# Spreading rows of 1/rms and norm weights over the partitions: two products of 512 columns with split diagonals instead of four float32 products of 128

## The chip, the cores and the metric

The kernel runs on one core of a Trainium2 chip. The metric is the device time of one execution in microseconds, the median of several runs. The engines are called TensorE (PE in the rows; PEld is its weight load), VectorE (DVE), ScalarE (ACT), GpSimd (POOL) and SyncE (SP, which here only issues transfers). L308 is line 308 of the kernel before.

## What is computed

The reference is a trunk of two layers over two groups of tokens, `x_sample` (512 tokens) and `x_prompt` (1024 tokens), 1024 features wide, all in float32:

```python
def rms_norm(x, g):
    xf = x.astype(jnp.float32)
    y = xf * lax.rsqrt(jnp.mean(xf * xf, axis=-1, keepdims=True) + EPS)
    return (y * g.astype(jnp.float32)).astype(x.dtype)

def run_trunk(x):
    cos, sin = axial_rope_tables(x.shape[1])
    for i in range(DEPTH):  # 2
        j = i // 2
        if i % 2 == 0:
            x = x + fourier_mixer(x, norm_mix[i], fourier_w[j])
        else:
            x = x + attention_mixer(x, norm_mix[i], attn_w_qkv[j], attn_q_norm[j],
                                    attn_k_norm[j], attn_w_o[j], cos, sin)
        x = x + swiglu_ffn(x, norm_ffn[i], ffn_w_gate[i], ffn_w_up[i], ffn_w_down[i])
    return x
```

Each mixer and each feed-forward block begins with `rms_norm`; the attention also normalises every head of Q and K.

## The kernel before

The tokens stand in three blocks of 512: block 0 is the sample, 1 and 2 are the prompt. Inside the trunk a block is held with its features on the 128 partitions (8 chunks `dc` of 128) and its 512 tokens along the free axis. The feed-forward inner width is 2816, 22 chunks of 128.

Products of float32 matrices are made from two float32r parts each. `split` (lines 235 to 244) writes a high part with ScalarE, rounded to float32r, and a low part, source minus high part, with VectorE or GpSimd; with a gain, ScalarE multiplies by it and the low part is one `scalar_tensor_tensor`. `mm3` (lines 246 to 249) then runs three matmuls, high by high, high by low, low by high, into the same bank; these are the rows of L247, L248 and L249. Weights are loaded by SyncE, their high part is made by ScalarE (L278) and their low part by GpSimd (L279).

The norm is spread over partitions as follows. A sum of squares of the 512 tokens becomes a column: `rstd_cols` gives a tile `y` of 128 x 4, token by token on the partitions, by way of twelve small VectorE instructions (`rsqrt`, lines 281 to 293). What multiplies the block is a row, 512 tokens along the free axis, the same on all partitions. `in_rows` (line 302) makes that row: for each of the four columns of `y`, ScalarE scales the identity by it (a diagonal matrix, L307), and TensorE multiplies the diagonal by a matrix of ones (L308), in float32, 128 columns at a time, into one PSUM bank `r`. The diagonals are tiles of the rotating tag `t`, of which the main chain has 3 buffers (`tF`), the side chain 4 (`tX`) and `moving` 6 (`tT`); the same tags hold loaded chunks of the residual, squares, rotated heads and results on their way to memory.

`in_rows` is called: twice at the start for the gains of the Fourier mixer, and twice more for the prompt's; once at the end of the sample's mixer (`follow`, the row is copied to `first["r"]` and multiplies the gate and up products of the first feed-forward block); at the head of `normed` (line 339), which makes the split operand `h` of the next block, six times; in `qkv` for each of two K heads of three blocks (line 1030); and in `moving` (line 796), which makes the operands of the last stage, for two blocks.

The work runs as a main chain and a side chain. The main chain is the feed-forward loop of one block (`ffn`), the side chain prepares the next block: the prompt's mixer, Q, K and V, attention, output projection, norms. `weave` advances the two by turns by costs in microseconds that are written at the `yield`s, and a scheduler then lays out each engine's queue from what is ready, with the program's order as priority. `pinned` keeps an instruction in program order. The last stage (`ffn_pair`) runs the second layer's feed-forward for blocks 1 and 2 alone and calls `in_rows` nowhere. At the start `busy(36)` runs 36 products of ones by ones to warm TensorE.

Of the kernel before, what the change touches and what calls it, by code (L numbers as in the profile page):

```python
# [10 lines left out]
F32 = mybir.dt.float32  # L11
F32R = mybir.dt.float32r
I32 = mybir.dt.int32
AF = mybir.ActivationFunctionType
# [3 lines left out]
P = 128  # L18
D = 1024
NC = D // P  # L20
TB = 512
# [103 lines left out]
def trunk_kernel(ctx: ExitStack, tc: tile.TileContext, t: dict):  # L125
    nc = tc.nc
    act, dve, pool, pe, sp = nc.scalar, nc.vector, nc.gpsimd, nc.tensor, nc.sync

    cp = ctx.enter_context(tc.tile_pool(name="cp", bufs=1))
# [4 lines left out]
    def open_pool(name, **kw):  # L134
        opened[name] = tc.tile_pool(name=name, bufs=1, **kw)
        pools[name] = opened[name].__enter__()
        return pools[name]

    def close_pool(name):
        opened.pop(name).__exit__(None, None, None)  # L140
# [17 lines left out]
    def nm(s):  # L158
        uid[0] += 1
        return f"{s}_{uid[0]}"  # L160

    def tl(name, shape, dt, tag, pool_=None):
        pool_ = pool_ or pools["sbX" if tag[-1] in "XB" else "sbF"]
        return pool_.tile([P, *shape], dt, tag=tag, name=nm(name), bufs=BUFS[tag])
# [23 lines left out]
    def bank():  # L188
        return tl("c", [TB], F32, "c" + cur[0], pools["ps" + cur[0]])

    def bank2():
        return tl("a", [2, TB], F32, "gX", pools["psX"])
# [20 lines left out]

    ident = cp.tile([P, P], F32, name="ident")
    make_identity(nc, ident)
    ones = cp.tile([P, P], F32, name="ones")
    dve.memset(ones, 1.0)
    act.activation(col(1), ones[:, 0:1], AF.Square)
    gains = cp.tile([P, 34], F32, name="gains")
# [16 lines left out]
    def split(hi, lo, src, gain=None, eng=None):  # L236

        eng = eng or dve
        if gain is None:
            act.copy(hi, src)  # L240
            eng.tensor_tensor(lo, src, hi.bitcast(F32), op=ALU.subtract)  # L241
        else:
            act.activation(hi, src, AF.Copy, scale=gain)
            eng.scalar_tensor_tensor(lo, src, gain, hi.bitcast(F32), op0=ALU.mult, op1=ALU.subtract)
# [57 lines left out]
    def in_rows(y, temp=None, ps=None):  # L302

        r = bank() if ps is None else ps
        for j in range(4):
            dg = (temp or tmp)(P)
            act.activation(dg, ident, AF.Copy, scale=y[:, j : j + 1])  # L307
            pe.matmul(r[:, j * P : (j + 1) * P], ones, dg, start=True, stop=True)  # L308
        return r

    ss, rstd, resident = {}, {}, {}
# [23 lines left out]
    def normed(b, gain, got, ab, held=None):  # L335

        yield 2.0
        r = in_rows(rstd[b])
        h = h_tile(ab)
        yield 1.0  # L340
        for dp in range(NC // 2):
            for dc, ps in zip((2 * dp, 2 * dp + 1), sides()):
                if held is None:
                    x = tmp()
                    sp.dma_start(x, xres[b][:, dc, :])
                else:
                    x = held[dc]
                dve.tensor_tensor(ps, r, x, op=ALU.mult)
                split(h[:, 0, dc], h[:, 1, dc], ps, gain=gain[:, dc : dc + 1])
            yield 1.5  # L350
        got["h"] = h
# [66 lines left out]
    def mixer(seq, done, u, xrs, zz):  # L418
# [4 lines left out]
        if two:  # L423
            g2 = bank2()
            ga, gb = in_rows(gx[:, 0:4], ps=g2[:, 0]), in_rows(gx[:, 4:8], ps=g2[:, 1])
            sums = [x.rearrange("p (k n) -> p k n", k=2) for x in whole[seq]]
        else:
            ga, gb = done["gain"]
            sums = [h[:, i] for h in (tl("x", [2, 2, TB], F32, "wX") for _ in range(2)) for i in range(2)]
# [362 lines left out]
    def moving(blocks, gain, ops):  # L792

        tp = open_pool("tT")
        yield 2.0
        r = [in_rows(rstd[b], lambda n: tl("t", [n], F32, "tT", tp)) for b in blocks]
        yield 1.0
        for j in range(4):
            v = {}
            for k in range(2):  # L800
                for d in range(2):
                    c = 4 * d + j
                    x = tl("x", [TB], F32, "tT", tp)
                    sp.dma_start(x, xres[blocks[k]][:, c, :])
                    v[d, k] = x
            a2 = bank2()
            a, b = a2[:, 0], a2[:, 1]
            for (d, k), x in v.items():
                dve.scalar_tensor_tensor(
                    a if (d, k) == (0, 1) else x, x, gain[:, 4 * d + j : 4 * d + j + 1], r[k], op0=ALU.mult, op1=ALU.mult  # L810
                )

            def put(name, src, eng=None):
                split(ops[name][:, 0, j], ops[name][:, 1, j], src, eng=eng)

            def put_late(k, src):
                x = tl("l", [2, TB], F32R, "lT", tp)
                split(x[:, 0], x[:, 1], src, eng=pool)
                sp.dma_start(late[:, k, :, j, :], x.bitcast(F32))

            put("B11", v[0, 0], pool)
            put("B21", v[1, 0], pool)
            yield 6.0
            dve.tensor_tensor(b, a, v[0, 0], op=ALU.subtract)
            put("T1", b)
            dve.tensor_tensor(v[0, 1], v[1, 1], a, op=ALU.subtract)
            put_late(0, v[0, 1])
            put("B22", v[1, 1], pool)
            yield 6.0
            dve.tensor_tensor(b, v[1, 1], b, op=ALU.subtract)  # L830
            put("T2", b)
            dve.tensor_tensor(v[0, 0], v[1, 0], b, op=ALU.subtract)
            put_late(1, v[0, 0])
            yield 6.0
        close_pool("tT")
# [408 lines left out]
    def aux_3():  # L1244
        yield from paced(qkv(2, kept[2]), 0.4)
        yield from paced(attend((1, 2)), 0.65)
        for b in (1, 2):
            yield from paced(out_projection(b), 0.5)
        close_pool("ap")
        close_pool("sbX")  # L1250
        tp = open_pool("mT")
        for name in ("B11", "B21", "T2", "T1", "B22"):
            ops[name] = tl(name, [2, 4, TB], F32R, "mT", tp)
        yield from moving((1, 2), g_ffn[1], ops)
        close_pool("psX")
        last["pair"] = ffn_pair(1, (1, 2), ops, t["y"])
        cur[0] = "F"
        v = next(last["pair"])
        cur[0] = "X"
        yield v  # L1260
# [102 lines left out]
```

## Time and profile before

| | us |
|---|---|
| median of 3 runs | 3044.05 (3040.32 to 3046.63) |
| the profiled execution | 3041.73 |
| its span, first to last instruction | 3040.0 |
| TensorE with a matmul in flight | 2967.5 (98%) |
| VectorE busy | 1667.8 (55%) |
| GpSimd busy | 1282.6 (42%) |
| ScalarE busy | 1231.3 (41%) |

A share of busy time is a mean over stages. Matmuls overlap, so the pace of TensorE is read from the distance of starts and not from durations. A row of the timeline gives start, duration, engine, line, operation, what it writes and reads, the shape, the count of instructions merged in it, and in brackets the idle time of the engine before it and what ended that. An instruction that waits for a semaphore at the head of its queue holds all that is queued behind it on that engine.

### The profile page before, as it was taken

How to read it: one execution, taken by the hardware profiler on the slowest of the kernel's cores; microseconds unless marked ns; L12 is line 12 of the kernel's file. 1: busy time of each engine (PE TensorE's matmuls, PEld its weight loads, DVE VectorE, ACT ScalarE, POOL GpSimd, SP SyncE). 2: the span in 40 equal slices, each digit the busy share in tenths (PEclk: the TensorE clock that was granted, in tenths of full speed). 3: DMA queues.
4: the chain of work that ended last, by engine and by line, in shares of the span. 5: the costliest groups of instructions: out<-in, count | busy, mean ns of one | idle time of the engine just before them, and what ended most of it. 6: DMA issues, size and time to landing. Idle time of an engine off the chain costs nothing. (4 is left out here: it accounts for less than half of the span.)

```text
span 3040.0 us, 36889 instructions
## 1 busy us (share of the span) xinstructions
PE 2967.5 (98%) x14184; PEld 2435.7 (80%) x14184; DVE 1667.8 (55%) x2883; ACT 1231.3 (41%) x1835; POOL 1282.6 (42%) x652
## 2 busy tenths in 40 slices
PE   7999999999999999999999999999999999999999
PEld 6778888888877788888878788877787787887777
DVE  7785565634556543533474465665236555655566
ACT  5533332423466522333344577776324222222221
POOL 4334444433333644444433311313636644645452
PEclk9999999999999999999999999999999999999999
DMA  6434543332232633433343211212635411111111
GB/s 223 150 111 132 166 139 104 125 104 77 97 98 90 229 131 133 141 106 101 99 142 111 87 59 53 75 51 91 221 121 183 164 56 54 44 56 55 44 55 63
DMA packets 132080, 330.05 MB, mean 109 GB/s; under 512 B 14176, under 2 KB 28512, under 8 KB 131264
## 3 DMA queue, kind: packets, MB, share of 16 engines
q1 hardware_dynamic: 130688, 318.71, 32.3%
q0 software_dynamic: 928, 7.94, 0.7%
q8 instruction: 111, 1.82, 0.3%
q10 hardware_dynamic: 288, 1.05, 0.1%
q14 instruction: 65, 0.53, 0.1%
HBM read 280.45 MB, written 47.19 MB: 108 GB/s over the span
## 5 line engine op out<-in xcount | busy, mean ns | idle before, releaser
L279 POOL TENSOR_TENSOR w<-raw,w 128x1024 fp32r<-128x1024 f32 x354 | 847.2, 2404 | 1308.1 <-ACT w L278 1259.2
L745 DVE TENSOR_TENSOR acc<-c,acc 128x512 f32<-128x512 f32 x704 | 483.0, 689 | 441.4 <-PE c L249 437.3
L278 ACT CAST w<-raw 128x1024 fp32r<-128x1024 f32 x354 | 371.2, 1050 | 562.3 <-PE c L249 270.9
L247 PE MATMUL g<-h,w 128*128 128x512 f32 x1408 | 556.5, 395 | 4.4 <-ACT t L777 4.4
L249 PE MATMUL g<-h,w 128*128 128x512 f32 x1408 | 552.8, 393 | 0.8 <-POOL w L279 0.8
L248 PE MATMUL g<-h,w 128*128 128x512 f32 x1408 | 552.3, 393 | 0.0
L247 PE MATMUL c<-mid,w 128*128 128x512 f32 x1056 | 417.6, 397 | 13.0 <-DVE acc L745 8.8
L248 PE MATMUL c<-mid,w 128*128 128x512 f32 x1056 | 414.2, 392 | 1.8 <-DVE mid L241 1.8
L249 PE MATMUL c<-mid,w 128*128 128x512 f32 x1056 | 413.6, 392 | 0.0
L241 POOL TENSOR_TENSOR w<-raw,w 128x512 fp32r<-128x512 f32 (+1 forms) x178 | 239.6, 1368 | 311.0 <-ACT w L240 290.0
L858 DVE TENSOR_TENSOR acc<-c,acc 128x512 f32<-128x512 f32 x352 | 240.8, 689 | 186.4 <-PE c L249 185.5
L247 PEld LDWEIGHTS g<-h,w 128*128 128x128 f32 x1408 | 265.6, 189 | 57.5 <-ACT t L777 5.4
L249 PEld LDWEIGHTS g<-h,w 128*128 128x128 f32 x1408 | 265.6, 189 | 56.5 <-POOL w L279 1.8
L248 PEld LDWEIGHTS g<-h,w 128*128 128x128 f32 x1408 | 265.7, 189 | 52.0
L247 PEld LDWEIGHTS c<-mid,w 128*128 128x128 f32 x1056 | 198.1, 188 | 75.1 <-DVE acc L745 18.5
L248 PEld LDWEIGHTS c<-mid,w 128*128 128x128 f32 x1056 | 198.9, 188 | 42.0 <-DVE mid L241 3.8
L249 PEld LDWEIGHTS c<-mid,w 128*128 128x128 f32 x1056 | 198.6, 188 | 40.4
L248 PE MATMUL c<-h,w 128*128 128x512 f32 x480 | 188.2, 392 | 3.1 <-POOL h L241 2.9
L247 PE MATMUL c<-h,w 128*128 128x512 f32 x480 | 189.1, 395 | 0.0
L240 ACT CAST w<-raw 128x512 fp32r<-128x512 f32 (+1 forms) x178 | 107.5, 648 | 196.9 <-PE a L249 79.8
L249 PE MATMUL c<-h,w 128*128 128x512 f32 x480 | 187.0, 390 | 0.0
L1073 DVE TENSOR_REDUCE col<-a 128x1 f32<-128x1024 f32 (+1 forms) x96 | 100.4, 1046 | 127.4 <-PE a L249 127.1
(342 smaller groups left out, 4765.5 us busy)
## 6 DMA issues: line engine op xcount, KB each, us to landing
raw<-in_down_dram SPq DMA_DIRECT2D x110, 512.0 KB, 3.5
raw<-in_gate_dram SPq DMA_DIRECT2D x88, 512.0 KB, 3.5
raw<-in_up_dram SPq DMA_DIRECT2D x88, 512.0 KB, 3.6
raw<-in_qkv_dram SPq DMA_DIRECT2D x36, 512.0 KB, 3.9
t<-xres SPq DMA_DIRECT2D x56, 256.0 KB, 3.9
raw<-in_wo_dram SPq DMA_DIRECT2D x24, 512.0 KB, 3.7
raw<-in_gate_dram SPq DMA_DIRECT2D x44, 256.0 KB, 2.6
raw<-in_up_dram SPq DMA_DIRECT2D x44, 256.0 KB, 3.1
```

Source lines behind the costliest of these rows:

```text
L240: act.copy(hi, src)
L241: eng.tensor_tensor(lo, src, hi.bitcast(F32), op=ALU.subtract)
L247: pe.matmul(out, lh, rh, start=first, stop=False)
L248: pe.matmul(out, lh, rl, start=False, stop=False)
L249: pe.matmul(out, ll, rh, start=False, stop=last)
L278: pinned(act.copy(flat[:, 0], raw)) if early else act.copy(flat[:, 0], raw)
L279: pool.tensor_tensor(flat[:, 1], raw, flat[:, 0].bitcast(F32), op=ALU.subtract)
L745: dve.tensor_tensor(acc[dc], ps, acc[dc], op=ALU.add)
L858: dve.tensor_tensor(acc, ps, acc, op=ALU.add)
L1073: dve.tensor_reduce(st[:, 0:1], s_in, op=ALU.max, axis=AX.X)
```

## The change

`ones` becomes a float32r tile that is also read as float32. In `in_rows` the four diagonals are no longer multiplied one by one in float32. Each is split into a high and a low part: ScalarE writes identity × column into the high part (float32r), VectorE writes identity × column − high part into the low part. The four high parts stand side by side in one tile of 512 columns, the four low parts in a second, both of tag `t`. Two float32r matmuls of 512 columns with the matrix of ones, one for each tile, add up in the bank `r`. All calls of `in_rows` take this way; in `moving` the helper that hands out tiles takes the type as well.

```diff
-    ones = cp.tile([P, P], F32, name="ones")
+    ones_r = cp.tile([P, P], F32R, name="ones")
+    ones = ones_r.bitcast(F32)
     dve.memset(ones, 1.0)
@@
         r = bank() if ps is None else ps
+        dg = [(temp or tmp)(TB, F32R) for _ in range(2)]
         for j in range(4):
-            dg = (temp or tmp)(P)
-            act.activation(dg, ident, AF.Copy, scale=y[:, j : j + 1])
-            pe.matmul(r[:, j * P : (j + 1) * P], ones, dg, start=True, stop=True)
+            js = slice(j * P, (j + 1) * P)
+            split(dg[0][:, js], dg[1][:, js], ident, gain=y[:, j : j + 1])
+        for b in range(2):
+            pe.matmul(r, ones_r, dg[b], start=b == 0, stop=b == 1)
         return r
@@
-        r = [in_rows(rstd[b], lambda n: tl("t", [n], F32, "tT", tp)) for b in blocks]
+        r = [in_rows(rstd[b], lambda n, dt: tl("t", [n], dt, "tT", tp)) for b in blocks]
```

## Rows read from the trace of the kernel before

**Rows 1.** The page: its head and the engines' busy time.

```profile
span 3040.0 us, 36889 instructions
...
PE 2967.5 (98%) x14184; PEld 2435.7 (80%) x14184; DVE 1667.8 (55%) x2883; ACT 1231.3 (41%) x1835; POOL 1282.6 (42%) x652
```

**Rows 2.** Waits of TensorE: us in total, times, longest us.

```profile
PE a L247 <- ACT p L1077: 12.5, 9, 1.7
...
PE c L308 <- ACT t L307: 6.4, 3, 5.1
```

**Rows 3.** Instructions of L307: count, ns min/median/max, first and last start in us.

```profile
L307 ACT ACTIVATE t<-ident,rs x36: 384/391/404, 101.7 to 2273.3; 128x128 f32<-128x128 f32 x36
...
L307 ACT ACTIVATE t<-ident,yk x24: 386/396/406, 738.4 to 1686.2; 128x128 f32<-128x128 f32 x24
L307 ACT ACTIVATE t<-ident,gains x16: 386/401/409, 4.7 to 114.4; 128x128 f32<-128x128 f32 x16
```

**Rows 4.** Timeline of TensorE at 24 us, the sample's mixer: start, us, what.

```profile
24.05 0.47 PE L640 MATMUL c<-wm,eo 128*96 128x512 f32 x1 [1.62 <-ACT wm L622]
```

**Rows 5.** Timeline at 1002 us, the products of one call unbroken.

```profile
1002.04 0.39 PE L248 MATMUL c<-mid,w 128*128 128x512 f32 x1
...
1002.27 0.40 PE L249 MATMUL c<-mid,w 128*128 128x512 f32 x1
...
1002.50 1.05 PE L308 MATMUL c<-t,ones 128*128 128x128 f32 x8
...
1003.31 0.47 PE L247 MATMUL g<-h,w 128*128 128x512 f32 x1
...
1003.62 0.39 PE L248 MATMUL g<-h,w 128*128 128x512 f32 x1
```

**Rows 6.** Timeline at 738 us, a K head's call with its products broken up.

```profile
738.37 1.42 ACT L307 ACTIVATE t<-ident,yk 128x128 f32<-128x128 f32 x4 [4.98 <-DVE yk L293]
...
738.73 0.39 PE L247 MATMUL g<-h,w 128*128 128x512 f32 x1
...
738.96 0.64 PE L308 MATMUL c<-t,ones 128*128 128x128 f32 x4
...
739.68 0.65 PE L308 MATMUL c<-t,ones 128*128 128x128 f32 x4
...
740.39 0.39 PE L249 MATMUL c<-h,w 128*128 128x512 f32 x1
```

**Rows 7.** Timeline of TensorE at 106 us, the first feed-forward chunk.

```profile
105.90 0.83 PE L308 MATMUL a<-t,ones 128*128 128x128 f32 x6
...
109.22 0.50 PE L247 MATMUL g<-h,w 128*128 128x512 f32 x1 [2.48 <-ACT t L777]
```

**Rows 8.** Timeline at 408 and 1524 us, the last diagonal and its product.

```profile
408.06 0.40 ACT L307 ACTIVATE t<-ident,rs 128x128 f32<-128x128 f32 x1 [3.47 <-DMA xres<-t]
...
408.51 0.49 PE L308 MATMUL c<-t,ones 128*128 128x128 f32 x2 [0.46 <-ACT t L307]
...
1523.88 0.49 PE L308 MATMUL c<-t,ones 128*128 128x128 f32 x2 [0.87 <-ACT t L307]
```

**Rows 9.** Instructions of three VectorE lines: ns min/median/max, first and last start.

```profile
L491 DVE SCALAR_TENSOR_TENSOR col<-x_p,m,col x2: 204/206/209, 184.1 to 185.5; 128x8 f32<-128x8 f32 x2
...
L453 DVE SCALAR_TENSOR_TENSOR t<-x_p,m,a x2: 730/732/734, 177.7 to 199.1; 128x512 f32<-128x512 f32 x2
...
L1074 DVE TENSOR_TENSOR col<-col,nrqc x96: 147/159/2364, 801.4 to 2109.7; 128x1 f32<-128x1 f32 x96
```

**Rows 10.** Timeline at 197 us, VectorE beside GpSimd.

```profile
196.79 4.76 POOL L279 TENSOR_TENSOR w<-raw,w 128x1024 fp32r<-128x1024 f32 x2 [5.03 <-ACT w L278]
196.86 2.36 DVE L491 SCALAR_TENSOR_TENSOR col<-x_p,r_p,col 128x8 f32<-128x8 f32 x1
```

**Rows 11.** Timeline at 1518 us, GpSimd and the diagonals of one call.

```profile
1516.22 4.76 POOL L279 TENSOR_TENSOR w<-raw,w 128x1024 fp32r<-128x1024 f32 x2 [4.24 <-ACT w L278]
...
1518.61 0.98 ACT L307 ACTIVATE t<-ident,rs 128x128 f32<-128x128 f32 x3
```

## Prediction

> **What bounds the kernel now.** I read the page first: TensorE has a matmul in flight for 2967.5 of 3040.0 us, 98% [rows 1], so what counts is TensorE's own time and the few gaps in its queue. The profiled execution took 3041.73 us, 1.7 us more than its span and 0.08% under the median of the runs, 3044.05; the sum below is a difference and is set on the median. I read the waits of TensorE next: the largest is 12.5 us in nine waits for the softmax's exponential, and the matmuls of line 308, which the change rewrites, waited 6.4 us in three places, 5.1 of it the first microseconds of the kernel [rows 2]. Then the lines that the change touches: 36 + 24 + 16 = 76 ScalarE diagonals [rows 3], four to a call, so 19 calls of `in_rows`. Two stand at the very start, 17 behind microsecond 100. In the first stage TensorE is not the bound: at 24 us it still sits idle 1.62 us for an operand that comes from loads by way of three other engines [rows 4]. I count the first two calls at nothing, with ±0.5 us for the warming matmuls behind them.
>
> **What the products cost now.** Each float32 product stands in the trace as two passes of 128 columns, eight passes to a call. Where the eight run unbroken, the matmul before them starts at 1002.27 and the second one after them at 1003.62: 1.35 us for what takes two steps of 0.23 us without them, so the call costs TensorE 0.89 us [rows 5]. Where the queue puts other matmuls between them it is dearer: from 738.73 to 740.39 are 1.66 us, with three ordinary steps of 0.23 us in it (the matmul at 738.73 and one behind each group of four), so 0.97 us [rows 6]. Of the 17 calls 3 run unbroken and 14 broken: 3 × 0.89 + 14 × 0.97 = 16.3 us.
>
> **What the new products cost.** Two products of 512 columns in float32r have the shape and the type of every matmul around them, and those start 0.23 us apart [rows 5]: 17 × 2 × 0.23 = 7.8 us. The trace shows nothing better than this pace. The worst near row is the first matmul behind the old passes, whose step is 0.31 us [rows 5]; both products at that would cost 10.5 us. I take 0.23, since all operands are as in the stream. The gain is 16.3 − 7.8 = 8.5 us, at the low end 5.8. One call gives part of it back: six of its passes, at 105.90, run just before a 2.48 us wait of TensorE for ScalarE's SiLU [rows 7]; what is cut there only lengthens the wait. About 0.4 us are lost, which leaves 8.1 us.
>
> **ScalarE and buffers.** ScalarE still makes four 128-wide copies of the scaled identity to a call, of the same shape, only rounded to float32r: no change. The call now takes two buffers of the rotating tag `t` and not four. In before the fourth diagonal had to wait for a buffer whose contents were still on the way to memory: ScalarE stood 3.47 us, and TensorE 0.46 us behind it at 408.51 and 0.87 us at 1523.88 [rows 8]. With two buffers those waits should go: 1.3 us more, bounds 0 and 1.3. The loads that follow in `normed` take buffers of the same tag; two are free earlier than before, two as late as before, and the activations that they feed are off the end's path. I count this at nothing; cover is the chunk by chunk feed-forward work that TensorE has ready in the meantime.
>
> **The new work on VectorE.** Each call adds four `scalar_tensor_tensor` of 128 × 128 (low part = identity × gain − high part), and the second product needs the last of them. Their own time: a form with all operands in SBUF took 0.21 us at 8 columns, one of 512 columns, with an operand in PSUM, took 0.73 [rows 9]; by width, 0.21 + 0.52 × 120/504 = 0.33 us (an estimate), 68 × 0.33 = 22 us on an engine that is busy 55% of the span [rows 1]. Cover is the idle 45%. Queued behind a piece on VectorE are the additions into `acc`, which give TensorE its output banks back; 0.33 us later they are still ahead of the need in most places, and without that cover the 22 us would stand on the path.
>
> What does not fit is this. The same 8-column form that took 0.21 us took 2.36 us at 196.86, right behind the start of a GpSimd subtraction of 2.4 us, and ended with it [rows 10]. The one-column product of line 1074, also SBUF with SBUF, runs from 147 to 2364 ns [rows 9]; I matched its 96 instances with GpSimd's: the 62 that met no GpSimd work took 147 to 161 ns, and nearly all of the long ones lie inside one. Forms with one operand in PSUM show nothing of the kind. The new pieces read `ident` and the high part and write the low part, all in SBUF. So a piece that meets a GpSimd subtraction waits for its end, up to 2.4 us, holds VectorE's queue meanwhile, and the second product holds TensorE's.
>
> How often? GpSimd is busy 42% of the span [rows 1]. I set four pieces, 0.31 us apart, behind the first diagonal of each of the 17 calls in the trace of before, and let each wait for a GpSimd subtraction then under way. Eleven calls meet none: ScalarE, which feeds GpSimd, has mostly stood waiting for the 1/rms column (4.98 us at 738.37 [rows 6]), so GpSimd has run dry by then. Six meet one. The pair at 1518.61 is such: the piece is ready at 1519.0, the second of two subtractions from 1516.22 ends at 1520.98, and the fourth piece is 1.9 us late [rows 11]. The six are 1.65, 1.61, 0.70, 1.18, 5.1 and 1.91 us late. The 5.1 is of a call whose products run tens of microseconds after its diagonals, so it counts nothing; the other five sum to 7.05 us, less a slack of some 0.3 us each that TensorE's queue left between diagonal and product: 5.5 us. The bounds: 0 if the queues leave room everywhere, and, if GpSimd were met at random, 0.42 × 17 = 7.1 calls of up to 2.4 us each, 17 us.
>
> The Trainium skill has this as a rule (SBUF — State Buffer, "SBUF: two separate sides" and "Who interferes with whom"): a VectorE instruction with two SBUF inputs and a GpSimd instruction that reads SBUF exclude each other, and the one that comes second blocks fully. The trace agrees: 2.36 us in place of 0.21 [rows 9, 10].
>
> **Sum.** −8.1 (products) − 1.3 (buffers) + 5.5 (pieces behind GpSimd) = −3.9 us, on the median 3040.1; on the profiled execution 3037.8.
>
> **The rivals.** (1) The pieces find GpSimd idle. The scheduler lays the instructions anew, and with two buffers a call begins directly when its column is ready, as the one at 738 does, where ScalarE has waited and GpSimd is drained. Then 1.5 us at most remain: −8.1 − 1.3 + 1.5 = −7.9 us, 3036. For it: eleven of 17 calls. Against it: six did meet GpSimd, and a ScalarE that no longer waits for buffers feeds GpSimd sooner.
> (2) Slower: GpSimd is met at its share and in full, 17 us, so −9.4 + 17 = +7.6 us, 3051.7. One mechanism, VectorE's piece behind GpSimd's subtraction with TensorE waiting on the second product. It decides for slower from 9.4 + 6.1 = 15.5 us on, 0.9 us for each of the 17 calls. For it: a piece that gets through lets the next subtraction in ahead of the following piece, so one call may pay twice; and a held VectorE also delays `acc`. Against it: the place by place count gives a third of that.
> (3) The change does less than it says: the products run at 0.31 us and the buffer waits stay, as another load takes the freed buffer: −5.4 + 5.5 = 0, 3044.
> (4) The order is laid out anew far from the calls (the eight passes stand between other matmuls in ever different ways, so it is not the text's order). The waits for the exponential are 12.5 us in nine places [rows 2]; a third more or less is ±4 us. This widens each case and is no case of its own.
>
> **How the numbers follow.** What a measurement of this kernel can tell from no change is about 0.2%, 6.1 us. The forecast with its pieces between 3.3 and 15.5 us late in sum stays within that: chance 0.39. Rival 3 also: 0.04. Rival 1: 0.41. Rival 2: 0.16. So faster 0.41, same 0.43, slower 0.16. The forecast's own range, with ±4 us of rival 4, is 3036 to 3046; the faster case reaches to −9.4 − 4, and I cut at 3032; upward the slower case's middle is the end, 3051.
>
> **What would show it.** Line 308 must show 38 matmuls of 512 columns in place of 152 passes, with next starts 0.23 us apart; busy time of TensorE should fall by about 8 us. The new VectorE group at the line of `split` (L244) with 128 × 128 should have a median near 0.33 us and some members of 1 to 2.4 us; the waits of TensorE should hold a new row, line 308's product for VectorE's low part, of 3 to 8 us. If that row is absent, rival 1 holds; above 15 us, rival 2. If line 308 still waits for ScalarE's diagonals at 0.5 us and more, the buffer term is wrong. If none of the small forms on VectorE is stretched beside GpSimd, the step on which the forecast differs from a plain gain of 9 us was wrong.

## The result and the profile after

The changed kernel took 3049.59 us (median of ten runs, 3046.55 to 3053.23) against 3042.68 us for the kernel before (ten runs, 3038.26 to 3046.63). The ratio is 1.0028, with a 95% interval of 1.0020 to 1.0035: slower, by 6.9 us between the medians. (The recorded ratios are taken over the single runs; the two medians alone give 1.0023.) The forecast was 3.9 us faster. The profiled execution took 3052.9 us. Its page, head and engines:

```profile
span 3051.1 us, 36728 instructions
...
PE 2965.2 (97%) x14070; PEld 2430.6 (80%) x14070; DVE 1704.4 (56%) x2959; ACT 1229.8 (40%) x1835; POOL 1283.4 (42%) x652
```

Against [rows 1], TensorE was busy 2.3 us less and idle 13.4 us more (span less busy time: 85.9 us, before 72.5). VectorE gained 36.6 us of work.

The lines have shifted by a few: the products of `in_rows` are now L311, ScalarE's high part L244, VectorE's low part L245. I call the 76 instructions of 128 × 128 on L245 the pieces (the line's wider ones are older work). The products, by line of the trace (count, ns min/median/max):

```profile
L311 PE MATMUL c<-t,ones x34: 389/396/795, 5.9 to 2285.1; 128*128 128x512 f32 x34
...
L311 PE MATMUL a<-t,ones x4: 496/628/628, 109.9 to 115.5; 128*128 128x512 f32 x4
```

Timeline of TensorE at 1000 us, one call between ordinary matmuls:

```profile
1000.64 0.39 PE L250 MATMUL c<-mid,w 128*128 128x512 f32 x1
1000.87 0.62 PE L311 MATMUL c<-t,ones 128*128 128x512 f32 x2
1001.33 0.40 PE L248 MATMUL g<-h,w 128*128 128x512 f32 x1
```

38 products are there, and a pair takes 1001.33 − 1000.87 = 0.46 us, two steps of 0.23, where the eight passes took 0.89 [rows 5]. This half of the change does what it says.

The pieces, by line (count, ns min/median/max):

```profile
L245 DVE SCALAR_TENSOR_TENSOR t<-ident,rs,t x36: 333/343/2425, 104.2 to 2284.7; 128x128 fp32r<-128x128 f32 x36
L245 DVE SCALAR_TENSOR_TENSOR t<-ident,yk,t x24: 339/345/1686, 738.7 to 1683.2; 128x128 fp32r<-128x128 f32 x24
...
L245 DVE SCALAR_TENSOR_TENSOR t<-ident,gains,t x16: 340/351/1885, 5.0 to 113.6; 128x128 fp32r<-128x128 f32 x16
```

The median is near the estimated 0.33 us, but nine pieces, in seven of the 17 calls behind 84 us, took 1.3 to 2.4 us: 16.6 us together, 13.5 more than nine ordinary ones. Waits of TensorE (us in total, times, longest):

```profile
PE a L248 <- ACT p L1080: 11.4, 9, 1.8
PE c L311 <- DVE t L245: 7.7, 4, 3.4
...
PE c L311 <- ACT t L244: 7.1, 3, 5.9
...
PE a L311 <- DVE t L245: 0.6, 1, 0.6
```

The second and the last row are new: TensorE waits for pieces, 8.3 us in five places. The third is almost all at the start (5.92 and 0.94 us); behind 100 us it holds 0.2 us, and the buffer waits of [rows 8] are gone.

The worst place is at 2279 us. Timeline of all engines there:

```profile
2279.01 4.76 POOL L280 TENSOR_TENSOR w<-raw,w 128x1024 fp32r<-128x1024 f32 x2 [11.30 <-ACT w L279]
...
2279.53 4.40 DVE L245 SCALAR_TENSOR_TENSOR t<-ident,rs,t 128x128 fp32r<-128x128 f32 x2 [0.47 <-ACT t L244]
...
2280.65 0.40 PE L311 MATMUL c<-t,ones 128*128 128x512 f32 x1
...
2283.85 0.69 DVE L781 TENSOR_TENSOR g<-g,t 128x512 f32<-128x512 f32 x1
2284.45 0.60 DVE L245 SCALAR_TENSOR_TENSOR t<-ident,rs,t 128x128 fp32r<-128x128 f32 x2
...
2285.10 0.50 PE L311 MATMUL c<-t,ones 128*128 128x512 f32 x1 [3.38 <-DVE t L245]
```

GpSimd begins the first of two subtractions half a microsecond ahead of the first piece. That piece ends only with the subtraction (2.05 us in place of 0.34), the second subtraction gets in ahead of the second piece, and that piece waits for the whole of it (2.43 us). VectorE has done two pieces in 4.40 us and has the multiplication of L781 and two more pieces to do; TensorE stands 3.38 us. What the clock does then, in three stretches (us; PE, PEld, DVE, ACT, POOL busy with counts; granted clock; DMA share, GB/s):

```profile
1547.20:2377.70 830.50, 793.27 (x4038) 652.71 (x4036) 446.02 (x769) 448.94 (x647) 298.55 (x146) 0.98 0.32 107
2281.00:2285.00 4.00, 0.72 (x4) 0.26 (x2) 4.00 (x5) 0.75 (x2) 2.78 (x2) 1.00 0.00 0
2286.00:2289.00 3.00, 3.00 (x9) 2.31 (x8) 2.51 (x4) 1.24 (x2) 1.74 (x2) 0.50 0.81 262
```

Behind the wait the granted clock is 0.50, the 1.2 GHz level: matmuls of 512 columns start 0.43 us apart there, and 0.23 apart again from 2289.3 us on.

To see where the time lies I cut each trace at the starts of the 1st, 176th, 352nd, 528th and 704th addition into `acc` and summed, stage by stage, the gaps of TensorE between matmuls and the time at the lower clock (from the clock records; the last stage leaves out some 3.9 us behind the last matmul):

| Stage | before: length, idle, half clock (us) | after | e9, below |
|---|---|---|---|
| start | 117.2, 21.1, 17.1 | 118.5, 24.4, 20.5 | 115.8, 23.2, 20.5 |
| additions 1 to 176 | 432.2, 6.8, 3.4 | 430.4, 7.6, 0.0 | 430.9, 6.6, 3.4 |
| 176 to 352 | 514.6, 7.8, 0.0 | 513.5, 8.0, 0.0 | 512.9, 7.8, 0.0 |
| 352 to 528 | 486.1, 1.0, 0.0 | 484.9, 1.2, 0.0 | 483.8, 0.2, 0.0 |
| 528 to 704 (1550 to 2365 us in before) | 815.0, 26.9, 6.8 | 830.5, 37.2, 27.3 | 819.8, 31.1, 20.5 |
| end | 674.9, 4.9, 1.4 | 673.4, 3.7, 0.8 | 674.0, 4.1, 2.0 |

In these executions the three middle stages each gained 1.1 to 1.8 us, 4.1 together, where nine calls at some 0.5 us and the buffer waits of [rows 8] would be 5.8; the start lost 1.3 and the stage behind 1550 us lost 15.5. Of the 15.5 us, 10.3 are idle TensorE; the rest is a slower pace, with 20.5 us more at half clock.

### The profile page after: what moved, and what is told of

It is laid out like the page before. It is cut to its first block, busy times and chain, and to the rows that moved or that the text cites. A ratio compares the mean times of both kernels' runs of the same rounds, so it can differ in the third digit from the quotient of the medians.

```text
span 3051.1 us, 36728 instructions
## 1 busy us (share of the span) xinstructions
PE 2965.2 (97%) x14070; PEld 2430.6 (80%) x14070; DVE 1704.4 (56%) x2959; ACT 1229.8 (40%) x1835; POOL 1283.4 (42%) x652
## 4 chain that ended last, share of the span: by engine, by line
PE 84%; DVE 4%; issue 3%; POOL 2%; ACT 2%; DMA 2%; SPq 0%; POOLq 0%; ACTq 0%; DVEq 0%
PE c L248 12%; PE c L249 12%; PE c L250 12%; PE g L250 10%; PE g L248 10%; PE g L249 10%; PE a L248 5%; PE a L250 5%; PE a L249 5%; PE c L1094 2%; POOL w L280 1%; DVE col L1077 1%; PE c L1027 1%; DMA raw<-in_down_dram 1%; ACT p L1080 1%
```

## The experiments

The theory after the result is the mechanism of rival 2: a piece with both inputs in SBUF waits for a GpSimd subtraction, TensorE waits for the piece. The rivals: the order laid out anew far from the calls; the longer start; VectorE held up as such, so that other work is late; the buffers. Each result is the median against the kernel before in the same job, with the ratio's 95% interval. A difference from the changed kernel is one between medians of different jobs, in which the kernel before had medians of 3040.94 to 3042.85 us. The excerpts are cut from `in_rows` unless another place is named.

**The piece with one operand in PSUM.** The high part is copied twice, once into the product's own bank, and the piece reads it there; ScalarE has four more copies per call.

```diff
-            split(dg[0][:, js], dg[1][:, js], ident, gain=y[:, j : j + 1])
+            act.activation(r[:, js].bitcast(F32R), ident, AF.Copy, scale=y[:, j : j + 1])
+            act.activation(dg[0][:, js], ident, AF.Copy, scale=y[:, j : j + 1])
+            dve.scalar_tensor_tensor(dg[1][:, js], ident, y[:, j : j + 1], r[:, js], op0=ALU.mult, op1=ALU.subtract)
```

> Each high part is written twice by ScalarE, once into the operand tile and once into the bank r, and VectorE's low part reads it from the bank. So VectorE does the same 76 pieces, but each with one operand in PSUM; ScalarE does four more copies a call (0.31 us each). Theory A (the loss is VectorE's pieces waiting for GpSimd's subtractions, all operands in SBUF): no piece above 0.5 us, the waits of TensorE for the low part fall from 8.3 us to under 2 us, and the time falls from 3049.6 to 3036 to 3043. Theory B (the loss is a queue order laid out anew, with other waits far from the calls): the time stays within 4 us of 3049.6, with pieces of 0.34 us. Theory C (the work on VectorE itself, 26 us more): stays at 3049 or above.

3040.37 us, ratio 0.9994 (0.9985 to 1.0002), 9.2 us less than the changed kernel. The pieces of one column and the wait, by line and in the list of waits:

```profile
L311 DVE SCALAR_TENSOR_TENSOR t<-ident,rs,c x36: 336/344/351, 104.8 to 2276.5; 128x128 fp32r<-128x128 f32 x36
```

```profile
PE c L313 <- DVE t L311: 12.7, 2, 7.6
...
PE a L313 <- DVE t L311: 1.2, 1, 1.2
```

None of the 76 pieces is stretched; the slowest took 351 ns. The waits of TensorE for pieces did not fall under 2 us as expected: they are 13.9 us, two at the very start and one of 1.2 us at 107 us, all in the first stage, which is 3.9 us longer than before with the added ScalarE work in it. Behind 120 us there is none. So the same instruction with the same arithmetic is not stretched once one input is out of SBUF, and the whole kernel is no longer slower.

**No low part.** Both products take the high part, so the rows hold twice that and VectorE has no pieces.

```diff
-            split(dg[0][:, js], dg[1][:, js], ident, gain=y[:, j : j + 1])
+            act.activation(dg[0][:, js], ident, AF.Copy, scale=y[:, j : j + 1])
         for b in range(2):
-            pe.matmul(r, ones_r, dg[b], start=b == 0, stop=b == 1)
+            pe.matmul(r, ones_r, dg[0], start=b == 0, stop=b == 1)
```

> No low part at all: both products of 512 columns take the high part, so TensorE does the changed kernel's work and VectorE that of before; the row comes out as twice the high part. Theory A: all of the gain shows, 9 us under before less the start's 1 us, 3033 to 3037. Theory B: between 3043 and 3052. Theory C: as A.

3038.01 us, ratio 0.9987 (0.9977 to 0.9996), above the expected 3033 to 3037. Without pieces the kernel gains 4.0 us, not the 8 to 9 that products and buffers promised. The queue of TensorE is another one here, so the order could be at work; e9 below keeps the queue up to 1550 us.

**The low part on ScalarE.** A column gains − high part is made once, and ScalarE writes eight diagonals to a call.

```diff
+        act.copy(r[:, 0:4].bitcast(F32R), y[:, 0:4])
+        dve.tensor_tensor(yl, y[:, 0:4], r[:, 0:4], op=ALU.subtract)
...
+            act.activation(dg[1][:, js], ident, AF.Copy, scale=yl[:, j : j + 1])
```

> The low part comes from ScalarE: the column is rounded into the bank, VectorE makes the low column (128 x 4, one operand in PSUM, 0.17 us), ScalarE makes eight diagonals in place of four. Two products of 512 columns as in the change. Theory A: 3034 to 3042, with a chain some 1.5 us longer to each call. Theory B: anywhere between 3040 and 3052. Theory C: as A.

3039.57 us, ratio 0.9994 (0.9985 to 1.0002): no slowdown without the pieces, and no clear gain.

**One float32 product of 512.** The kernel before, with one diagonal buffer and one product to a call; nothing is split.

```diff
+        dg = (temp or tmp)(TB)
         for j in range(4):
-            dg = (temp or tmp)(P)
-            act.activation(dg, ident, AF.Copy, scale=y[:, j : j + 1])
-            pe.matmul(r[:, j * P : (j + 1) * P], ones, dg, start=True, stop=True)
+            act.activation(dg[:, j * P : (j + 1) * P], ident, AF.Copy, scale=y[:, j : j + 1])
+        pe.matmul(r, ones, dg, start=True, stop=True)
```

> Before, with the four float32 diagonals side by side in one tile and one float32 product of 512 columns in place of four of 128: no split, no piece on VectorE, one buffer. If a float32 pass goes by columns (111 ns for 128), its two passes take 0.9 us and only the breaks between matmuls go, some 1 us in all, plus the buffer waits of 1.3 us: 3039 to 3043 under theories A and C. Theory B: within 5 us of before on either side, with no relation to those sums.

3038.32 us, ratio 0.9985 (0.9977 to 0.9994): of the kernels that compute the whole reference, the one with the largest gain over the kernel before. Timeline of TensorE:

```profile
999.20 0.40 PE L249 MATMUL c<-mid,w 128*128 128x512 f32 x1
999.43 1.02 PE L308 MATMUL c<-t,ones 128*128 128x512 f32 x2
999.89 0.79 PE L247 MATMUL g<-h,w 128*128 128x512 f32 x1
1000.52 0.40 PE L248 MATMUL g<-h,w 128*128 128x512 f32 x1
```

From 999.43 to 1000.52 are 1.09 us with one ordinary step of 0.23 in it: 0.86 us to a call, where the passes of 128 took 0.89 unbroken [rows 5] and 0.97 broken [rows 6]. The products save 14 × 0.11 + 3 × 0.03 = 1.6 us, with the buffer waits of [rows 8] some 3.0 of the 3.7 us measured (3039 to 3043 had been expected).

**The late calls as before.** From the last side chain on (five calls), `in_rows` works as in the kernel before; the others as changed.

```diff
+        if late_calls:
+            for j in range(4):
+                dg = (temp or (lambda n, dt: tmp(n)))(P, F32)
+                act.activation(dg, ident, AF.Copy, scale=y[:, j : j + 1])
+                pe.matmul(r[:, j * P : (j + 1) * P], ones, dg, start=True, stop=True)
+            return r
...
     def aux_3():
+        late_calls.append(1)
```

> The changed kernel, but the five calls of its last side chain (norm and two K heads of block 2, two in the preparation of the last stage) make the row as before, with four float32 products. In the changed kernel's trace the stretch that holds them lost 15.5 us and the stretch up to 1550 us had gained 2.8. Theory A (pieces behind GpSimd, here 1.2 and 3.4 us of TensorE's waits, and the clock that falls behind the second): the loss of that stretch goes, 3037 to 3042. Theory B (the order, laid out anew by any change of durations): 3043 to 3050, since the order behind 1550 us is again another one.

3039.79 us, ratio 0.9988 (0.9979 to 0.9997): 9.8 us less than the changed kernel. In its profiled execution the stage behind 1550 us takes 815.1 us with 10.2 us at half clock, where the changed kernel had 830.5 and 27.3. Five calls carry most of the loss.

**Pieces that no one reads.** The kernel before, with the 76 pieces added and their results unused.

```diff
+        lo = (temp or tmp)(TB)
...
+            dve.scalar_tensor_tensor(lo[:, js], ident, y[:, j : j + 1], dg, op0=ALU.mult, op1=ALU.subtract)
```

> The kernel before with its float32 products, and beside them the 76 low pieces on VectorE, all operands in SBUF, into a tile that no one reads. TensorE waits for none of them; they only hold VectorE. Theory A as first put (TensorE waits for the piece): 3041 to 3045. If holding VectorE (late additions into acc, late column chains) is the larger part: 3046 to 3052. Theory B: anywhere in 3038 to 3050.

3050.81 us, ratio 1.0024 (1.0014 to 1.0034): slower though TensorE needs no piece. The edit does not do what it was meant to: each piece reads a diagonal, so holds its buffer, and the next diagonal waits for that. The wait shows in the list of waits of TensorE:

```profile
PE c L311 <- ACT t L309: 14.2, 13, 4.5
```

Seven of the 13 lie in the first 14 us, 7.6 us, and six behind 100 us, 6.6 us, where the kernel before had two of 1.3 us together. Ten of its pieces are stretched. So pieces behind GpSimd can reach TensorE by way of buffers too; on holding VectorE alone it says nothing.

**The start as before.** The two calls at the very start as in the kernel before.

```diff
-    got_s["gain"] = in_rows(gx[:, 0:4]), in_rows(gx[:, 4:8])
+    got_s["gain"] = in_rows(gx[:, 0:4], old=True), in_rows(gx[:, 4:8], old=True)
```

> The changed kernel with its first two calls as before. In the trace of the changed kernel these end 1.3 us later and the warming matmuls queue behind them: 1.3 us less than the changed kernel, 3048. Theory B: within 5 us of it on either side.

3051.86 us, ratio 1.0026 (1.0016 to 1.0036), where 3048 had been expected. The start fell by 1.8 us in the profiled execution, the whole did not get shorter. The longer start is not what made the change slow. The wait of 3.38 us is there again, at 2286.77 us, and the stage behind 1550 us takes 828.5 us.

**One wide piece.** The low column as in e3, kept in the bank, and all four low diagonals in one VectorE product of 512 columns that reads it from PSUM.

```diff
+        dve.tensor_tensor(r[:, 8:12], y[:, 0:4], r[:, 0:4], op=ALU.subtract)
...
+        dve.tensor_tensor(
+            dg[1].rearrange("p (j n) -> p j n", j=4),
+            ident.unsqueeze(1).broadcast_to([P, 4, P]),
+            r[:, 8:12].unsqueeze(2).broadcast_to([P, 4, P]),
+            op=ALU.mult,
+        )
```

> Repair: the column's low part is made in the bank r (ScalarE rounds the column into it, VectorE subtracts, 128 x 4), and one VectorE product of 512 columns, identity by that column, writes all four low diagonals; its column operand lies in PSUM. ScalarE keeps its four high diagonals. Theory A: no stretched VectorE instruction in it, no wait of TensorE for it above 0.7 us; 3034 to 3040. Theory B: 3036 to 3050.

3041.29 us, ratio 0.9996 (0.9988 to 1.0005): no stretched piece (at most 690 ns for 512 columns) and no slowdown, but the gain of the products does not arrive whole (3034 to 3040 was expected); which part of the edit takes it was not told apart.

**A piece with one SBUF input.** The piece becomes a reduction over single elements of the high diagonal: same place, same wait for ScalarE, same buffers, but one input. The rows hold twice the high part. Up to 1550 us the queue of TensorE is that of the changed kernel but for five neighbours that change places.

```diff
-            split(dg[0][:, js], dg[1][:, js], ident, gain=y[:, j : j + 1])
+            act.activation(dg[0][:, js], ident, AF.Copy, scale=y[:, j : j + 1])
+            dve.tensor_reduce(dg[1][:, js], dg[0][:, js].bitcast(F32).unsqueeze(2), op=ALU.max, axis=AX.X)
```

> The changed kernel with one thing replaced: VectorE's piece is a reduction over a group of one of the high part alone (128 x 128, one SBUF input), so the second tile holds the high part again and the row comes out as twice the high part. Count, size, place and dependence of the pieces stay, and TensorE's queue is that of the changed kernel up to about 1550 us but for five neighbours that change places. Theory A: no piece above 0.5 us, no wait of TensorE for a piece above 0.5 us behind 100 us; up to 1550 us some 2 us less than the changed kernel, the whole 3036 to 3043. Theory B: up to 1550 us as the changed kernel, the whole anywhere in 3038 to 3052. Theory C (VectorE's added work): as the changed kernel, 3049.

3033.82 us, ratio 0.9980 (0.9970 to 0.9990): by the medians 8.4 us faster than before and 15.8 faster than the changed kernel. The median flatters it: six of the eleven runs lie at 3031.8 to 3033.8 us and five at 3038.0 to 3047.0, and the median is the highest of the six. By the recorded ratios it is 6 us faster than before and 14.6 faster than the changed kernel. The pieces by line, and the same place as above in the timeline:

```profile
L309 DVE TENSOR_REDUCE t<-t x76: 269/277/290, 4.6 to 2274.7; 128x128 fp32r<-128x128 f32 x76
```

```profile
2273.08 4.79 POOL L280 TENSOR_TENSOR w<-raw,w 128x1024 fp32r<-128x1024 f32 x2 [11.51 <-ACT w L279]
...
2273.33 0.87 DVE L309 TENSOR_REDUCE t<-t 128x128 fp32r<-128x128 f32 x3 [0.62 <-ACT t L309]
...
2274.72 0.28 DVE L309 TENSOR_REDUCE t<-t 128x128 fp32r<-128x128 f32 x1
...
2275.26 0.39 PE L311 MATMUL c<-t,ones 128*128 128x512 f32 x1
```

The same two subtractions run, all four pieces lie inside them, none takes longer than 0.3 us, and TensorE goes on. By their starts 25 of the 76 reductions fell into a GpSimd subtraction (26 of e1's 76 pieces, 11 of the changed kernel's): GpSimd is met all the same, and the price is gone. The Trainium skill (SBUF — State Buffer, "Who interferes with whom") says that a VectorE instruction with at most one SBUF input, outside its two-port modes, doesn't contend with GpSimd, and that a reduction never does on this chip. The 76 reductions, at most 290 ns, agree with both, and e1's 76 pieces, at most 351 ns, with the first.

**The last two calls as before.** Those of `moving` (`old=True` there).

> The changed kernel, but the two calls that prepare the last stage make the row as before. In the changed kernel's trace one of these pieces holds VectorE 4.4 us in sum, TensorE waits 3.38 us for it, and the clock stands at half for 3.4 us behind it. Theory A: 3.4 + 1.7 - 0.9 (dearer products) = 4.2 us less than the changed kernel, 3045.4. If the earlier three calls of that side chain are the cause: 3049 to 3051. Theory B: within 5 us on either side.

3043.28 us, ratio 1.0006 (0.9997 to 1.0015): 6.3 us less than the changed kernel, where 4.2 had been expected. That fits a wait of 3.38 us with a larger price than itself; but the queue behind it is another one too, so the size of that surplus is not shown.

**Holding VectorE alone.** The kernel before, with 76 one-column instructions that have two SBUF inputs and whose results no one reads.

```diff
+            dve.scalar_tensor_tensor(col(4)[:, 0:1], ident[:, 0:1], y[:, j : j + 1], ident[:, 0:1], op0=ALU.mult, op1=ALU.subtract)
```

> The kernel before with, for each diagonal, one more VectorE instruction of one column whose two tensor operands are both in SBUF, and which no one reads or waits for: 76 of 0.2 us that can only hold VectorE behind GpSimd. Theory A in its first form (only TensorE's direct wait for the piece counts): 3042 to 3044. If held VectorE alone delays the additions and the column chains: 3045 to 3050. Theory B: 3038 to 3048.

3042.26 us, ratio 1.0001 (0.9992 to 1.0010). By line:

```profile
L309 DVE SCALAR_TENSOR_TENSOR col<-ident,rs x36: 203/212/2340, 101.1 to 2273.1; 128x1 f32<-128x1 f32 x36
```

Only three of them took over 1 us, 4.6 us in sum, so they tested the held engine thinly; what they did meet cost nothing that can be measured.

**Two attempts at a better version.** The first: float32 products of 512 at the start and in the late calls, and e1's pieces in the twelve between.

> Repair: the two calls of the start and the five of the last side chain take one float32 product of 512 columns, the twelve between take two float32r products with the low part made from the bank, as in the first experiment. Sum of the stretches seen: start -1, up to 1550 us -5.8, behind it +2 to -1: 3034 to 3040 under theory A. Theory B: 3036 to 3047.

3039.12 us, ratio 0.9992 (0.9983 to 1.0000). The second: float32 products in the first three calls, and in the other sixteen the low column in the bank with four VectorE products of 128 that read it from PSUM.

```diff
+        dve.tensor_tensor(r[:, 8:12], y[:, 0:4], r[:, 0:4], op=ALU.subtract)
...
+            dve.tensor_tensor(dg[1][:, js], ident, r[:, 8 + j : 9 + j].broadcast_to([P, P]), op=ALU.mult)
```

> The first three calls take one float32 product of 512 columns, the 16 behind take two float32r products; the low column is made in the bank r (128 x 4), and four VectorE products of 128 x 128, identity (SBUF) by a low column (PSUM), write the low diagonals. So the pieces have the count and the size of the changed kernel's, and one SBUF input. If the ninth experiment's 8.4 us under before were the products and nothing else: 3033 to 3037. If half of it was a lucky order: 3036 to 3042, as the other repairs. If the low part costs by itself (one more small step before the products): 3040 and above, with waits of TensorE for the piece behind 100 us.

3040.47 us, ratio 0.9999 (0.9990 to 1.0008). Its pieces are never stretched:

```profile
L320 DVE TENSOR_TENSOR t<-ident,c x56: 274/279/289, 408.0 to 2276.6; 128x128 fp32r<-128x128 f32 x56
```

In the profiled execution all stages behind the start are together 7.4 us shorter than before; the cheaper products and the buffer waits are both in that. The start is 5.9 us longer; there the wait for SiLU has grown from 2.48 us [rows 7]. Timeline of TensorE:

```profile
115.07 0.80 PE L248 MATMUL g<-h,w 128*128 128x512 f32 x1 [4.52 <-ACT t L791]
```

The gain is made and lost again in another place. The time is in the range that was expected if half of e9's gain was a lucky order.

## Why the prediction was wrong

**Products: right by the pace.** The pair took 0.46 us as predicted. Predicted were −8.1 us, −9.4 with the buffers; e9, which has the products, the buffers and the pieces but not their meetings, gives −8.4 by its median and −6 by its ratio, e13 −7.4 behind the start. These hold an order of their own, so how near they come is in part luck. TensorE's busy time did not fall by 8 us but by 2.3; in e9 it fell by 7.1 (2960.4 us). By the table of stages it fell by 7.3 up to 1550 us (7.8 in e9) and rose by 5.2 behind (0.6 in e9), where the changed kernel has 20.5 us more at half clock. What failed there is the view, not the term: a matmul at half clock counts as longer busy (0.63 us against 0.39 behind 2286 us).

**Buffers: right in the trace, without a size of their own.** The waits of [rows 8], 1.33 us, are gone; one of 0.21 us, at 105 us, is the only wait for a diagonal behind 100 us. No run changes the buffers alone, so none gives the term by itself.

**The pieces behind GpSimd: right mechanism, mis-sized term.** This is the step that failed: the term of +5.5 us in the sum was too small by 9 to 10 us. It had 0 and 17 as bounds; the measured price is 15.8 us by e9 (14.6 by the recorded ratios), 9.2 by e1 and 9.8 by e5, which both contain losses of their own or other calls. So rival 2 was nearly what happened: its condition was 15.5 us, its time 3051.7, and 3049.59 was measured. I gave it 0.16 because the place by place count gave a third of its price. Rival 2's share of calls came out, seven met against its 7.1. The direct waits were indeed of the counted size: 1.71, 0.56, 1.20 and 3.38 us behind 100 us, 6.85 against 5.5. So the sign that was to tell the cases apart did not: the new row of waits was 8.3 us, just above the 3 to 8 of the forecast and far from the 15 that were to mean rival 2, and the time was rival 2's all the same. Three things were left out of the sum.

First, the place by place count stood on GpSimd's rows of before. The pair at 1518.61 [rows 11], counted at 1.91 us, gave TensorE no wait; the last call, at 2272 us in before and counted as clear, met two subtractions one behind the other and paid 3.38. That one call may pay twice the prediction named against itself, and put no number on it.

Second, a wait of TensorE was priced at its length. Timeline of an early meeting in the trace of after:

```profile
103.96 2.38 POOL L280 TENSOR_TENSOR w<-raw,w 128x1024 fp32r<-128x1024 f32 x1 [1.45 <-ACT w L279]
104.22 3.06 DVE L245 SCALAR_TENSOR_TENSOR t<-ident,rs,t 128x128 fp32r<-128x128 f32 x4 [1.37 <-ACT t L244]
...
107.33 0.50 PE L311 MATMUL c<-t,ones 128*128 128x512 f32 x1 [1.71 <-DVE t L245]
...
111.91 0.50 PE L248 MATMUL g<-h,w 128*128 128x512 f32 x1 [0.53 <-ACT t L780]
```

Here the 1.71 us are paid back: the wait for SiLU sank from 2.48 [rows 7] to 0.53. At 2285 nothing of the kind pays back, and the clock falls besides. Behind 1550 us, e9 is 10.7 us shorter than the changed kernel in the profiled executions: 4.6 are the two waits for pieces there (1.20 + 3.38), 1.5 other gaps, and 4.6 busy time, of which 6.8 us less at half clock explain some 3.4 (half of it, an estimate). So about half of that stage's price is not in the waits. Much of that half comes behind the last wait: by the starts of the 528th, 661st, 666th and 704th addition, 2.3 of the 10.7 us are lost up to 2273 us, 4.0 at the wait and 4.4 in the 86 us behind it.

Third, the whole run's clock. The ten runs of the changed kernel had granted clocks of 0.991 to 0.994, mean 0.9929; a straight line through them loses 1.8 us per 0.001 (2.2 from the fastest, 3046.55 us at 0.994, to the slowest, 3053.23 at 0.991). Those of the kernel before had 0.9948 on average, over the 110 runs in the experiments' jobs. By these slopes the lower clock is some 3 to 4 of the 6.9 us (an estimate), whether it follows from the waits or not. Against e9 it is less: at 0.994 the changed kernel took 3046.6 to 3049.8 us in four runs, e9 3033.0 to 3039.1 in three.

**The start: put at nothing, and longer.** Predicted at nothing, ±0.5; the first warming matmul starts 0.94 us later (10.92 us, 9.98 in before), and the whole first stage, with three later calls in it, is 1.3 us longer in the profiled execution. Timeline there:

```profile
9.06 0.69 DVE L399 TENSOR_TENSOR x<-c,x 128x512 f32<-128x512 f32 x1 [1.20 <-DMA x<-in_rows_s_dram]
9.67 0.61 DVE L245 SCALAR_TENSOR_TENSOR t<-ident,gains,t 128x128 fp32r<-128x128 f32 x2
...
10.33 0.79 PE L311 MATMUL c<-t,ones 128*128 128x512 f32 x1 [1.46 <-DVE t L245]
```

The last pieces of the second call queue on VectorE behind an addition that waits for a load. [Rows 4] show that TensorE is not the bound at 24 us; the warming matmuls behind the product are its work all the same. By e7 this is not what decided, and e9, with the same calls, has a first stage 1.4 us shorter than before, so the size is within what other things move there.

**The order: a wider term than ±4.** e1, e2, e3, e8, e9 and e13 all have the new products (e13 in 16 calls) and no stretched piece, and lie 1.7, 4.0, 2.5, 1.6, 8.4 and 0.5 us under the kernel before. Different ScalarE work and the start may explain part; the rest is put down to the queue laid out anew and the clock, which no run separates, spread over some 8 us. It is as large as the products' gain. Even so the order alone does not make the loss: none of these six is slower than before, and the three kernels that keep stretched pieces in the last calls, the changed one, e6 and e7, are 6.9 to 9.0 us slower.

What stays open: how the 15.8 us (or 14.6) divide exactly. The waits (6.85) and the start (1.3) are read from rows; that the falls of the clock are caused by these waits is argued from their places, as at 2285, and e9's profiled execution, whose clock fell almost as long (48.4 us in all, after 50.6, before 30.8), shows that they come without such waits too.

## What to carry to other kernels

Work put on VectorE on a path that TensorE waits for should have at most one input in SBUF when GpSimd streams beside it: an operand in PSUM or a one-input form took the price away, 9 to 16 us of 3040. A wait of the bounding engine can cost more than its length (behind the one of 3.38 us another 4.4 were lost against e9, with the clock at half in places, which is not shown to be its doing), and less where the next wait absorbs it; price the meetings at the whole GpSimd instruction, twice where two of them follow each other. And a saving of 0.3% on the bounding engine can vanish in a queue laid out anew, so keep the smallest edit that has it (here one float32 product, −3.7 us).

## What the hardware showed that I had not expected

- Two inputs in SBUF let the second GpSimd instruction in between: 2.05 and 2.43 us for two pieces of 0.34 in a row, where four reductions inside two subtractions took 0.87 us (three) and 0.28 (one).
- Behind a TensorE wait of 3.38 us in a stretch that is otherwise dense the granted clock was 0.50 from 2286 to 2289, at work without a gap (3.00 us busy of 3.00).
- Runs of one and the same kernel differ with the granted clock: 3046.55 us at 0.994, 3053.23 at 0.991.
- A float32 product of 512 columns took TensorE 0.86 us to a call as two passes, hardly less than eight passes of 128 (0.89).
